# The step-by-step state-space recurrence of a hybrid block, issued on VectorE instead of GpSimd

## The chip, the core and the metric

One core of a Trainium2 chip runs the whole kernel. The metric is the device time of one execution in microseconds (us). Its engines are TensorE (PE in the profile, with PEld for its weight loads), VectorE (DVE), ScalarE (ACT), GpSimd (POOL) and SyncE (SP), each of which works through its own queue of instructions in order; DMA queues are fed from SP, ACT and POOL.

## What is computed

The reference is one layer of a diffusion backbone on 256 context and 256 latent tokens of width 2048: a token mixer with three branches (a Hyena long convolution, a chunkwise mLSTM, and an S5 state-space model), merged and projected, and then an MLP. The change touches the S5 branch. Each of its 48 groups has 64 complex states that run over the tokens in both directions:

```
def s5_direction(u, ab_re, ab_im, bb_re, bb_im, c_re, c_im, x0, readout):
    bu_re = jnp.einsum('blgc,gpc->blgp', u, bb_re)
    bu_im = jnp.einsum('blgc,gpc->blgp', u, bb_im)
    ...
    _, _, s_re, s_im = lax.associative_scan(s5_combine, (a_re, a_im, bu_re, bu_im), axis=1)
    ...
    y = (jnp.einsum('blgp,gcp->blgc', s_re, c_re.astype(F32))
         - jnp.einsum('blgp,gcp->blgc', s_im, c_im.astype(F32)))
```

The scan is x[n] = A x[n-1] + B u[n], with A diagonal and complex.

## The kernel before

**Matrix products.** Every large product streams its weights from HBM in chunks of 128x1024 float32 (512 KB). A chunk is loaded by SP into a tile `wr` (four buffers). ACT rounds it into `wh` (line 190), DVE subtracts to get the rest, `wl` (line 194, function `split`); `wh` and `wl` have three buffers each. PE then multiplies with `wh` and `wl` (line 211): in the stage of this change a chunk feeds 24 matmuls of 128x256. A `wr` buffer can be loaded again when DVE has made its `wl`; a `wl` buffer can be written again when PE has used it.

**Side work.** Generators are woven into the chunks: after each chunk a side advances by a given rate. One side, `mod_late`, loads further 512 KB tiles of `w_mod` into the same `wr` buffers and accumulates them on DVE into `mac` (lines 1178 and 1180, two instructions for each tile). 

**The S5 branch.** Tokens are grouped by eight, so that 512 tokens give 64 columns (`NCH`). `s5_inject` writes all inputs of the recurrence into the tile `S` (a `t32` tile, `t` in the profile), 128 partitions by 2 directions x 2 parts (real, imaginary) x 24 x 64 columns; the column is innermost, so one column of `S` is 96 elements that lie 64 elements (256 bytes) apart. `s5_scan` (lines 642 to 655) then takes 63 steps of four instructions of 128x96 each. The temporaries `sc1` and `sc2` (both `sc` in the profile) are contiguous. `s5_output` reads the states into a block matrix `xb` (`b` in the profile; four copies by ACT and four products by DVE, line 679, for each of six column tiles), and PE reads `xb` with the matmuls of line 686.

**Where it runs.** In `run`, stage pB: six chunks of the Hyena projection (`hy`), `s5_inject`, then the scan as side 0 at rate 2, so that its 63 steps are woven into the next 32 chunks (30 of `hy`, 2 of the merge gates `mg`); 30 more chunks of `mg` are issued, then `s5_output` at rate 0.6 over the following 16 and more. At ends of blocks of `hy`, ACT copies the product out of PSUM, ACT and DVE apply a short convolution (lines 740 and 742), and POOL issues a DMA into `HX`; at ends of blocks of `mg`, ACT copies into `mg` tiles and POOL issues a DMA into `MG`.

**Order.** Within each engine the order of instructions is set when the kernel is built, by a scheduler that estimates how long each instruction takes on its engine. So an instruction that goes to another engine can also change the order of other work.

Of the kernel before, what the change touches and what calls it, by code (L numbers as in the profile page):

```python
# [115 lines left out]
class Kern:  # L116
# [526 lines left out]

    def s5_scan(self):

        v = self.nc.gpsimd
        S = self.S
        for n in range(1, NCH):
            t1 = self.t(self.sm, [P, 2, 2, 24], "sc1", 2)
            t2 = self.t(self.sm, [P, 2, 2, 24], "sc2", 2)  # L650
            v.tensor_mul(t1, self.a8[:, 0], S[:, :, :, :, n - 1])  # L651
            v.tensor_mul(t2, self.a8[:, 1], S[:, :, ::-1, :, n - 1])  # L652
            v.tensor_add(t1, t1, S[:, :, :, :, n])  # L653
            v.tensor_add(S[:, :, :, :, n], t1, t2)  # L654
            yield
# [917 lines left out]
```

## Time and profile before

| what | value |
|---|---|
| time, median of 3 runs | 2005.19 us (2005.02 to 2005.46) |
| the profiled execution, its time | 2014.18 us |
| the profiled execution, its span | 2012.4 us |
| mean granted TensorE clock | 0.966 |
| busy share of the span | PE 93%, PEld 85%, DVE 65%, ACT 40%, POOL 18% |

The profile is of one execution, 9 us above the median of the timed runs. All places below are in microseconds from the start of its span. A busy share is an average over stages with different limits.

### The profile page before, as it was taken

How to read it: one execution, taken by the hardware profiler on the slowest of the kernel's cores; microseconds unless marked ns; L12 is line 12 of the kernel's file. 1: busy time of each engine (PE TensorE's matmuls, PEld its weight loads, DVE VectorE, ACT ScalarE, POOL GpSimd, SP SyncE). 2: the span in 40 equal slices, each digit the busy share in tenths (PEclk: the TensorE clock that was granted, in tenths of full speed). 3: DMA queues.
4: the chain of work that ended last, by engine and by line, in shares of the span. 5: the costliest groups of instructions: out<-in, count | busy, mean ns of one | idle time of the engine just before them, and what ended most of it. 6: DMA issues, size and time to landing. Idle time of an engine off the chain costs nothing.

```text
span 2012.4 us, 34496 instructions
## 1 busy us (share of the span) xinstructions
PE 1870.4 (93%) x13945; PEld 1707.4 (85%) x13945; DVE 1300.5 (65%) x1810; ACT 803.2 (40%) x1063; POOL 361.7 (18%) x534
## 2 busy tenths in 40 slices
PE   5888999999997995999889998999999999999996
PEld 1666988989997995999779877999988899998985
DVE  8985777647866553556786866766755555555556
ACT  2433324226543333544234533444433344444332
POOL 1221101000019994000452400400000000000001
PEclk7898999999998997999999998999999999999998
DMA  9997667775797765677657866577765566666553
GB/s 346 339 344 262 192 202 220 227 208 174 232 349 230 239 222 210 226 254 259 244 180 253 276 225 227 158 240 224 254 224 187 187 183 186 181 186 231 190 188 105
DMA packets 253472, 455.92 MB, mean 227 GB/s; under 512 B 28597, under 2 KB 75349, under 8 KB 251776
## 3 DMA queue, kind: packets, MB, share of 16 engines
q1 hardware_dynamic: 221824, 382.43, 59.4%
q0 software_dynamic: 14112, 50.83, 7.0%
q10 hardware_dynamic: 17376, 20.45, 3.1%
q8 instruction: 109, 1.79, 0.4%
q14 instruction: 51, 0.42, 0.1%
HBM read 424.75 MB, written 32.05 MB: 227 GB/s over the span
## 4 chain that ended last, share of the span: by engine, by line
PE 67%; DMA 10%; DVE 9%; POOL 8%; issue 3%; ACT 2%; SPq 0%; ACTq 0%; POOLq 0%; DVEq 0%
PE mm L211 59%; PE aux L211 4%; DMA wr<-in_w_mod_dram 4%; DVE wl L194 3%; DMA wr<-in_w_in_dram 2%; POOL sc L651 2%; POOL sc L653 2%; POOL sc L652 2%; POOL t L654 2%; DMA wr<-in_w_out_dram 1%; ACT wh L190 1%; PE px L406 1%; PE px L211 1%; PE aux L214 1%; DVE mac L1180 1%
## 5 line engine op out<-in xcount | busy, mean ns | idle before, releaser
L211 PE MATMUL mm<-t,wh 128*128 128x256 f32 x5888 | 1101.7, 288 | 29.0 <-ACT wh L190 18.1
L211 PEld LDWEIGHTS mm<-t,wh 128*128 128x128 f32 x5888 | 932.2, 194 | 49.6 <-ACT wh L190 19.9
L194 DVE TENSOR_TENSOR wl<-wr,wh 128x1024 fp32r<-128x1024 f32 (+1 forms) x517 | 649.6, 1263 | 385.9 <-ACT wh L190 385.4
L190 ACT ACTIVATE wh<-wr 128x1024 fp32r<-128x1024 f32 (+1 forms) x517 | 545.9, 1058 | 811.0 <-PE mm L211 580.6
L211 PE MATMUL mm<-t,wl 128*128 128x256 f32 x2944 | 847.6, 288 | 13.9 <-DVE wl L194 13.8
L211 PEld LDWEIGHTS mm<-t,wl 128*128 128x128 f32 x2944 | 570.1, 194 | 25.9 <-DVE wl L194 18.3
L1180 DVE SCALAR_TENSOR_TENSOR mac<-wr,vecs,mac 128x512 f32<-128x512 f32 x240 | 185.3, 772 | 156.5 <-DMA wr<-in_w_mod_dram 153.8
L211 PE MATMUL mm<-wh,t 128*128 128x512 f32 (+1 forms) x960 | 249.1, 349 | 0.2
L211 PEld LDWEIGHTS mm<-wh,t 128*128 128x128 f32 x960 | 169.0, 190 | 24.2 <-ACT wh L190 1.6
L211 PE MATMUL mm<-wl,t 128*128 128x512 f32 (+1 forms) x480 | 168.0, 350 | 5.5 <-DVE wl L194 5.5
L211 PE MATMUL mm<-wh,ff 128*128 128x512 f32 (+1 forms) x576 | 155.3, 358 | 0.0
L211 PEld LDWEIGHTS mm<-wh,ff 128*128 128x128 f32 x576 | 101.7, 188 | 17.6
L211 PEld LDWEIGHTS mm<-wl,t 128*128 128x128 f32 x480 | 91.3, 190 | 20.5 <-DVE wl L194 9.2
L211 PE MATMUL mm<-wl,ff 128*128 128x512 f32 (+1 forms) x288 | 103.0, 357 | 0.0
L211 PE MATMUL mm<-ty,wh 128*128 128x256 f32 x384 | 73.3, 289 | 0.0
L1402 POOL DMA_DIRECT2D t<-in_ln_g_dram x1 | 0.5, 535 | 355.0 <-PE mm L211 355.0
L211 PE MATMUL mm<-ty,wl 128*128 128x256 f32 x192 | 56.4, 294 | 7.6 <-DVE wl L194 7.5
L211 PEld LDWEIGHTS mm<-wl,ff 128*128 128x128 f32 x288 | 54.2, 188 | 8.8
L211 PEld LDWEIGHTS mm<-ty,wh 128*128 128x128 f32 x384 | 60.7, 192 | 0.9
L406 PE MATMUL px<-wr,b 128*32 128x512 f32 x128 | 41.4, 739 | 18.1 <-DVE s5t L335 10.5
L211 PE MATMUL aux<-t,t 128*128 128x384 f32 (+3 forms) x160 | 47.3, 411 | 7.7 <-DVE t L1146 3.2
L211 PEld LDWEIGHTS mm<-ty,wl 128*128 128x128 f32 x192 | 36.9, 192 | 9.1 <-DVE wl L194 8.4
(384 smaller groups left out, 1621.6 us busy)
## 6 DMA issues: line engine op xcount, KB each, us to landing
wr<-in_w_ff_dram SPq DMA_DIRECT2D x256, 512.0 KB, 3.9
wr<-in_w_in_dram SPq DMA_DIRECT2D x192, 512.0 KB, 4.7
wr<-in_w_mod_dram SPq DMA_DIRECT2D x160, 512.0 KB, 4.8
wr<-in_w_out_dram SPq DMA_DIRECT2D x32, 512.0 KB, 4.7
wh<-in_w_mod_dram SPq DMA_DIRECT2D x16, 512.0 KB, 7.6
wl<-in_w_mod_dram SPq DMA_DIRECT2D x16, 512.0 KB, 7.1
QD<-s5Q POOLq DMA_DIRECT2D x12, 512.0 KB, 7.1
WA<-s5wa POOLq DMA_DIRECT2D x24, 256.0 KB, 6.2
```

The lines of the kernel that those rows point to most:

```text
L190: return self.nc.scalar.activation(out, in_, f, bias=bias, scale=scale)
L194: self.nc.vector.tensor_sub(lo, x, hi.bitcast(F32))
L211: self.nc.tensor.matmul(out, lhsT, rhs, start=start, stop=stop, skip_group_check=True)
L214: self.nc.tensor.transpose(out, in_, self.c("ident", n)[:, :n])
L406: nc.tensor.matmul(ps[o:o + 32], self.st[:, k, :], raw[:, kk, :], start=k < 4, stop=k >= KT - 4, skip_group_check=True, tile_position=(0, o))
L651: v.tensor_mul(t1, self.a8[:, 0], S[:, :, :, :, n - 1])
L652: v.tensor_mul(t2, self.a8[:, 1], S[:, :, ::-1, :, n - 1])
L653: v.tensor_add(t1, t1, S[:, :, :, :, n])
L654: v.tensor_add(S[:, :, :, :, n], t1, t2)
L1180: v.scalar_tensor_tensor(acc, x, c, acc, op0=ALU.mult, op1=ALU.add)
L1402: nc.gpsimd.dma_start(g2r, I["ln2_g"].to_broadcast([P, D]))
```

## The change

One line: the four instructions of each step of the scan go to VectorE.

```
     def s5_scan(self):
 
-        v = self.nc.gpsimd
+        v = self.nc.vector
         S = self.S
         for n in range(1, NCH):
             t1 = self.t(self.sm, [P, 2, 2, 24], "sc1", 2)
             t2 = self.t(self.sm, [P, 2, 2, 24], "sc2", 2)
             v.tensor_mul(t1, self.a8[:, 0], S[:, :, :, :, n - 1])
             v.tensor_mul(t2, self.a8[:, 1], S[:, :, ::-1, :, n - 1])
             v.tensor_add(t1, t1, S[:, :, :, :, n])
             v.tensor_add(S[:, :, :, :, n], t1, t2)
             yield
```

All 252 instructions leave POOL and stand on DVE, between its `wl`, `mac` and convolution instructions. Here are twelve rows of the DVE queue in the stage of `mg`, with the difference marked; `sc_...` are the scan's temporaries, `t_677` is `S`, `wl_7379` and `wl_7409` are two consecutive chunks.

```order
 L194 TENSOR_TENSOR wl_7379<-wr_7376,wh_7378 128x1024
+L651 TENSOR_TENSOR sc_814_6190<-t_677_5292 128x96
+L652 TENSOR_TENSOR sc_815_6191<-t_677_5292 128x96
+L653 TENSOR_TENSOR sc_814_6190<-sc_814_6190,t_677_5292 128x96
+L654 TENSOR_TENSOR t_677_5292<-sc_814_6190,sc_815_6191 128x96
+L651 TENSOR_TENSOR sc_816_6196<-t_677_5292 128x96
+L652 TENSOR_TENSOR sc_817_6197<-t_677_5292 128x96
+L653 TENSOR_TENSOR sc_816_6196<-sc_816_6196,t_677_5292 128x96
 L194 TENSOR_TENSOR wl_7409<-wr_7406,wh_7408 128x1024
-L1180 SCALAR_TENSOR_TENSOR mac_7371<-wr_7496,vecs_93,mac_7371 128x512 x2
+L654 TENSOR_TENSOR t_677_5292<-sc_816_6196,sc_817_6197 128x96
+L1180 SCALAR_TENSOR_TENSOR mac_7371<-wr_7496,vecs_93,mac_7371 128x512
```

Eight instructions of the scan come between the two chunks and their `mac` pair, and the pair is split. PE's queue moves too: where the first matmuls of `s5_output` (line 686) stood, the products of the chunk `wh_8472` (an `mg` chunk) now run on.

```order
 L211 MATMUL mm_8110<-t_20_103,wh_8389 128x256 x2
 L211 MATMUL mm_8110<-t_20_103,wl_8390 128x256
-L211 MATMUL mm_8110<-t_20_103,wh_8472 128x256
-L686 MATMUL aux_8200<-s5wq_8190,b_1109_8182 64x128 x16
-L692 MATMUL aux_8200<-s5tp_8188,b_1111_8186 32x128 x8
-L211 MATMUL mm_8110<-t_20_103,wh_8472 128x256
+L211 MATMUL mm_8110<-t_20_103,wh_8472 128x256 x2
 L211 MATMUL mm_8110<-t_20_103,wl_8473 128x256
 L211 MATMUL mm_8110<-t_20_103,wh_8472 128x256 x2
```

They stand 90 matmuls of 128x256 later, in the middle of the chunk `wh_8679`, where the fourth column tile of `s5_output` was before.

```order
 L211 MATMUL mm_8593<-t_20_103,wl_8680 128x256
 L211 MATMUL mm_8593<-t_20_103,wh_8679 128x256
-L211 MATMUL aux_8460<-consts_91,b_1110_8184 128x32 x8
-L686 MATMUL aux_8514<-s5wq_8504,b_1109_8182 64x128 x16
-L692 MATMUL aux_8514<-s5tp_8502,b_1143_8500 32x128 x8
+L686 MATMUL aux_8200<-s5wq_8190,b_1109_8182 64x128 x16
+L692 MATMUL aux_8200<-s5tp_8188,b_1111_8186 32x128 x8
 L211 MATMUL mm_8593<-t_20_103,wh_8679 128x256
 L211 MATMUL mm_8593<-t_20_103,wl_8680 128x256
```

Each of the other column tiles moves back by the same 90 matmuls. Counted from the last matmul of `s5_inject`, the first matmul of line 686 came after 1123 products before, and comes after 1213 now. ACT's copies into `xb` move with them; SP's queue is unchanged; POOL's queue keeps its DMAs in their order.

## Rows read from the trace of the kernel before

**Rows 1.** The page: 40 slices (busy, granted clock in tenths), chain shares by engine.

```profile
PE   5888999999997995999889998999999999999996
...
PEclk7898999999998997999999998999999999999998
...
PE 67%; DMA 10%; DVE 9%; POOL 8%; issue 3%; ACT 2%; SPq 0%; ACTq 0%; POOLq 0%; DVEq 0%
```

**Rows 2.** Waits, 560 to 850 us: engine, line, waited for; us in total, times, longest.

```profile
PE aux L686 <- POOL sc L651: 21.4, 1, 21.4
...
ACT wh L190 <- DMA HX<-b: 11.8, 1, 11.8
...
ACT mg L190 <- DMA MG<-mg: 6.3, 1, 6.3
```

**Rows 3.** Line 651: duration ns min/median/max, first and last start us, forms.

```profile
L651 POOL TENSOR_TENSOR sc<-t x63: 431/449/1454, 601.8 to 776.2; 128x96 f32<-128x96 f32 x63
```

**Rows 4.** Windows of 20 us: busy us and instructions by engine, PEclk, DMA share, GB/s.

```profile
600.00:620.00 20.00, 15.39 (x112) 14.90 (x111) 12.24 (x17) 8.68 (x14) 15.33 (x27) 0.85 0.74 254
...
660.00:680.00 20.00, 20.00 (x169) 20.00 (x168) 10.97 (x10) 8.36 (x9) 18.97 (x29) 1.00 0.75 237
...
760.00:780.00 20.00, 2.91 (x28) 2.94 (x30) 3.30 (x6) 3.76 (x9) 16.66 (x41) 0.52 0.07 27
```

**Rows 5.** Chain that ended last, in order of time: start us, us, what.

```profile
597.19 6.00 PE mm L211 x50
...
777.09 3.68 PE aux L686 x32
...
787.14 1.90 PE aux L686 x32
...
826.97 38.83 PE mm L211 x323
```

**Rows 6.** Timeline of DVE, a recurrence of 128x48 operations: start us, us, what.

```profile
14.98 0.24 DVE L477 TENSOR_TENSOR s5t<-s5pq 128x48 f32<-128x48 f32 x1
15.15 0.23 DVE L478 TENSOR_TENSOR s5t<-s5pq 128x48 f32<-128x48 f32 x1
15.42 0.24 DVE L479 TENSOR_TENSOR s5pq<-s5t 128x48 f32<-128x48 f32 x1
15.70 0.24 DVE L480 TENSOR_TENSOR s5t<-s5pq 128x48 f32<-128x48 f32 x1
15.86 0.23 DVE L481 TENSOR_TENSOR s5t<-s5pq 128x48 f32<-128x48 f32 x1
```

**Rows 7.** DVE by form, whole span: busy us, mean ns, idle before.

```profile
L725 DVE TENSOR_TENSOR z<-z,b 128x256 f32<-128x256 f32 x6 | 2.2, 418 | 0.0
...
L479 DVE TENSOR_TENSOR s5pq<-s5t 128x48 f32<-128x48 f32 x7 | 1.7, 245 | 0.2
...
L496 DVE TENSOR_TENSOR s5t<-s5t 128x48 f32<-128x48 f32 x1 | 0.2, 207 | 0.0
```

**Rows 8.** DVE by form, 600 to 780 us.

```profile
L194 DVE TENSOR_TENSOR wl<-wr,wh 128x1024 fp32r<-128x1024 f32 x47 | 64.8, 1406 | 21.5 <-ACT wh L190 21.5
```

**Rows 9.** Timeline of DVE, 830 to 900 us, where POOL computes nothing.

```profile
838.13 0.75 DVE L1180 SCALAR_TENSOR_TENSOR mac<-wr,vecs,mac 128x512 f32<-128x512 f32 x1 [1.77 <-DMA wr<-in_w_mod_dram]
838.79 1.22 DVE L194 TENSOR_TENSOR wl<-wr,wh 128x1024 fp32r<-128x1024 f32 x1
...
888.69 3.52 DVE L194 TENSOR_TENSOR wl<-wr,wh 128x1024 fp32r<-128x1024 f32 x3
```

**Rows 10.** Timeline of DVE around the first step of the recurrence.

```profile
601.54 0.35 DVE L641 TENSOR_TENSOR t<-aux,one 128x64 f32<-128x64 f32 x2
...
604.95 0.48 DVE L742 SCALAR_TENSOR_TENSOR b<-b,vecs,b 128x252 f32<-128x252 f32 x1
605.38 1.23 DVE L194 TENSOR_TENSOR wl<-wr,wh 128x1024 fp32r<-128x1024 f32 x1
```

**Rows 11.** DMA issues, 600 to 780 us: count, KB each, median us to landing.

```profile
wr<-in_w_mod_dram SPq DMA_DIRECT2D x14, 512.0 KB, 5.1
```

More of the change, by code (lines that the diff above doesn't have):

```diff
@@ L644, in s5_scan @@
     def s5_scan(self):
-        v = self.nc.gpsimd
+        v = self.nc.vector
         S = self.S
```

## The prediction

> **What bounds the kernel now.** First the page: PE is busy in nine tenths of most slices, and the chain that ended last runs 67% through PE, but 8% of it through POOL. One slice in the middle, the sixteenth, falls to 5 tenths [rows 1]. The waits of that stretch name the cause: PE stood 21.4 us before the first matmul of line 686, for the last step of the scan on POOL [rows 2]. The scan ran from 601.8 to 776.2 us [rows 3], and the windows show POOL busy for up to 19 of 20 us while PE does almost nothing from 760 to 780 and its granted clock averages 0.52 there [rows 4]. So here the scan on POOL ended last, not PE. Its median instruction takes 449 ns but its longest 1454 [rows 3].
>
> Two smaller losses of the stretch hang on the same queue. POOL also issues the DMAs of `HX` and `MG`; ACT waited 11.8 and 6.3 us for buffers that these DMAs were to free [rows 2], since they were queued behind scan instructions.
>
> **What is removed.** POOL computes nothing in the stretch any more, so the 21.4 us go as far as DVE is not as late, and the DMAs are issued when their data is there. The unit of comparison is the start of line 686: before, at 777.1 us [rows 5], after 1123 products of `mm`. The changed queue of PE puts it after 1213. A product takes 38.83/323 = 0.120 us on a full PE [rows 5], so before, the same amount of work was done at 777.1 + 90 x 0.120 = 787.9 us. The first set of 32 matmuls of line 686 took 3.68 us, a later one 1.90 [rows 5]: PE came out of the wait at half its granted clock (1.2 instead of 2.4 GHz). Without the wait 1.8 us more are won: **the mark to beat is 789.7 us**.
>
> **What is added on DVE.** The trace has no 128x96 instruction on DVE that steps through memory. The nearest is another recurrence, 128x48, whose elements lie 36 bytes apart: 245 ns, against 207 ns for a contiguous 128x48 [rows 7], so 37 ns for 48 elements, 0.78 ns each. A contiguous 128x256 takes 418 [rows 7], so 48 more elements cost 48 x (418 - 207)/208 = 49 ns. A scan instruction: 207 + 49 + 96 x 0.78 = **331 ns**. All four kinds have at least one operand in `S`, so all pay. From the starts in the same recurrence, an instruction that doesn't need the one just before it starts 0.16 to 0.17 us after it, 0.08 sooner than the duration; one that does starts 0.27 to 0.28 after it, 0.04 later [rows 6]. So 0.25 and 0.37 us from start to start.
>
> Counted in the changed order from the first scan instruction to the last product of line 679 for the first column tile:
> - 251 scan instructions, of which 74 are directly followed by one that needs them: 74 x 0.37 + 177 x 0.25 = 71.6 us.
> - 47 `wl` at 3.52/3 or a little less, 1.15 [rows 9]: 54.0. While POOL computed, they took 1406 ns each [rows 8], against 1.22 without it [rows 9]: this price is the one without.
> - 28 `mac` at 838.79 - 838.13 = 0.66 [rows 9]: 18.5.
> - 14 convolution instructions at 605.38 - 604.95 = 0.43 [rows 10]: 6.0.
> - eight small ones, priced as a scan instruction, 0.25: 2.0.
>
> Sum 152.1 us. DVE also waits. A `mac` pair needs its `w_mod` tile, whose load starts when DVE frees the `wr` buffer four tiles earlier, and takes 5.1 us [rows 11]. Six of the pairs stand only 3.4 to 4.1 us of DVE work behind that point (22.3 us together): 6 x 5.1 - 22.3 = 8.3 us. Behind the waiting `mac` stand the scan and the next `wl`, and PE waits for that. Together 160.4 us. The scan can start as before, after the last copy of line 641 at 601.9 [rows 10], so line 686 starts at about 762.5.
>
> PE alone would be there sooner: 1213 products from 597.2 us [rows 5], 145.6 us, and the 4.6 us that it stood at the end of a `hy` block between 600 and 620 [rows 4], which are ACT's and stay, with some 2 us of clock (0.85 in that window): 750 us. So **DVE becomes the bound of the stretch**, with 152 us of work in 160, and PE, some nine tenths busy, waits a little before most chunks. I take off 2 us more for the ends of the three `hy` blocks, where DVE cannot run ahead (nothing to 3 us). The gain: 789.7 - 762.5 - 2 = **25 us**. Afterwards PE is full up to 866 (38.83 us of products without a gap) [rows 5] and no DVE work is added, so nothing gives it back. From the profiled execution, 2014.2 - 25 = 1989; it was 9 us above the median of the runs, so the median goes from 2005.2 to **1980**.
>
> **The unknown price, from both sides.** `S` steps by 256 bytes, not 36. Below: if such steps cost nothing, a scan instruction takes 256 ns, the sum is 134 us and the waits some 10, and PE at 750 is the bound: gain 39, 1966. Above: as on POOL, 449 ns [rows 3], 0.37 and 0.49 from start to start: 101.8 us of scan, 182 with the rest, some 4 of waits: 788 us, gain 0 to 2. I take the value of the rows with the same kind of access on the same engine.
>
> The Trainium skill speaks against the change here (Vector Engine (DVE) Microarchitecture Reference, 5.2 Measured stream behaviour on trn2): a port keeps its full rate only for runs of at least two adjacent words; single words that hop cost about 1.7 ns each instead of 1.05, and in one case, a step of 24 words, 2.5. By its 1.7 the estimate is 0.32 us for an instruction, which the 128x48 rows bear out at 0.78 ns extra; by its 2.5 it is 0.40, and the time about 1993. No run yet shows which of them a step of 64 words pays.
>
> **The rivals.**
> 1. *PE stays the bound.* The steps are cheap or hidden, gain 33 to 39, 1966 to 1972. For it: contiguous rows of 207 ns. Against: every row with steps pays. Chance 0.10.
> 2. *The longer step costs more.* Halfway between 331 and 449 ns, 0.39: 0.31 and 0.43 from start to start, 86.7 us of scan, 167 with the rest, 6 of waits: 775, gain 13, 1992. Nothing in the rows excludes it. Chance 0.17.
> 3. *Slower: DVE is saturated.* The scan sits between `wl`s, which PE needs every 24 x 0.120 = 2.88 us; five of its instructions fall on each. Without them DVE needs 80.5 us for the stretch; to reach the mark at 789.7 it may take 187.8, so with 4 of waits 103 us are left for 251 instructions, 0.41 each from start to start, against 0.285 forecast. Beyond that the kernel is slower by 2.5 us for each 0.01: at 0.45, 10 us, 2015. For it: PE now hangs on DVE for 160 us, and a `mac` or convolution that waits holds up everything. Against: no DVE row of this size comes near. Chance 0.09.
> 4. *No change.* The time won is lost again later, or the price is as on POOL: 2005. Chance 0.04, since the stretch behind is PE's alone.
>
> **How the numbers follow.** The forecast has 0.60 (1976 to 1987), the rivals 0.10, 0.17, 0.09 and 0.04. 1980 is that of the likeliest case. A range of 1968 to 1996 leaves out half of rival 1 (0.05) and rivals 3 and 4 (0.13), and so 0.18. Faster by over 0.2% (4 us, about what a measurement of this kernel tells from no change): 0.60 + 0.10 + 0.17 = 0.87, less 0.01 for the edge of rival 2: 0.86. Same 0.05, slower 0.09.
>
> **What the changed profile would show.** No wait of PE for line 686 above 1 or 2 us; scan instructions on DVE with a mean near 0.33 us; DVE busy above 90% from 602 to 762; `wl` back at 1.23 us; many short waits of PE for `wl` (about 10 us in sum) with the clock still near 1; ACT's waits for `HX` and `MG` gone; line 686 first at 760 to 766, and the rest of the span shifted as a block. It is wrong if the scan's mean is above 0.4 us, if the short waits bring PE's clock down over the stretch, or if the wait for line 686 comes back with DVE as its releaser.

## The result, and the profile after

The median of the changed kernel is 1984.16 us (1979.80 to 1987.72, four runs) against 2005.11 (2004.02 to 2005.46, four runs): a ratio of 0.9896 with a 95% interval of 0.9879 to 0.9914. The forecast was 1980. The profiled execution after took 1979.8 us, the fastest of its four, while that of before took 2014 (in later comparisons the kernel before ran from 2000.6 to 2016.6 us), so spans are not compared below; stretches between the same instructions are.

The page of the changed kernel, the lines that answer to [rows 1]:

```profile
PE   5887999999998999999889998999999999999996
...
PEclk7888999999999999999999998999999999999998
...
PE 69%; DVE 13%; DMA 12%; issue 3%; ACT 2%; POOL 0%; ACTq 0%; POOLq 0%; DVEq 0%
```

The slice with 5 tenths is gone, and so is POOL's share of the chain; DVE's has grown from 9 to 13%.

The waits of the changed kernel from 560 to 850 us, against [rows 2] (engine, line, waited for; us in total, times, longest):

```profile
DVE mac L1180 <- DMA wr<-in_w_mod_dram: 28.0, 16, 8.8
...
PE mm L211 <- DVE wl L194: 8.2, 8, 1.5
...
PE mm L211 <- ACT wh L190: 3.2, 1, 3.2
PE aux L211 <- DVE z L701: 2.6, 1, 2.6
```

PE no longer waits for line 686, and ACT no longer for `HX` or `MG`. A wait of 2.6 us behind line 701 is new. The eight short waits for `wl` are not: the same view of the kernel before has, beside the 21.4 us for the scan,

```profile
PE mm L211 <- ACT wh L190: 8.4, 2, 5.3
...
PE mm L211 <- DVE wl L194: 6.4, 8, 1.4
```

So from the scan's start to line 686 PE stood 21.4 + 8.4 + 6.4 = 36.2 us before and 8.2 + 3.2 = 11.4 us after: 24.8 us less, while its waits for `wl` grew by only 1.8.

The scan and the output of the changed kernel by line (duration ns min/median/max, first and last start us), against [rows 3]:

```profile
L651 DVE TENSOR_TENSOR sc<-t x63: 317/332/344, 596.7 to 755.3; 128x96 f32<-128x96 f32 x63
...
L686 PE MATMUL aux<-s5wq,b x192: 272/273/418, 757.3 to 803.2; 128*64 128x128 f32 x192
```

DVE of the changed kernel by form, from the first scan instruction to the first of line 686 (busy us, mean ns, idle before), against [rows 8]:

```profile
L194 DVE TENSOR_TENSOR wl<-wr,wh 128x1024 fp32r<-128x1024 f32 x47 | 57.3, 1220 | 0.0
L1180 DVE SCALAR_TENSOR_TENSOR mac<-wr,vecs,mac 128x512 f32<-128x512 f32 x28 | 21.0, 749 | 10.8 <-DMA wr<-in_w_mod_dram 10.6
L651 DVE TENSOR_TENSOR sc<-t 128x96 f32<-128x96 f32 x63 | 20.9, 332 | 1.5
```

These are the terms of the forecast's sum: 47 `wl`, 28 `mac`, an instruction of 332 ns where 331 was forecast, waits for the modulation's tiles of 10.6 us where 8.3 was. Line 686 comes 757.3 - 596.7 = 160.6 us after the scan's start; 160.4 had been worked out. The chain that ended last, from 590 to 770 us, runs 33% through loads of `w_mod` tiles, 18% through `wl`, 18% through PE's products and 15% through the scan: DVE's queue ended last there, and its waits for `mac` tiles are the largest part of it.

Windows of the changed kernel, against [rows 4] (window, its length, then busy us and instructions of PE, PEld, DVE, ACT, POOL; PEclk, DMA share, GB/s):

```profile
660.00:680.00 20.00, 19.12 (x157) 18.92 (x158) 18.53 (x44) 8.40 (x9) 1.07 (x2) 1.00 0.74 234
...
760.00:780.00 20.00, 19.58 (x218) 18.56 (x217) 7.74 (x15) 11.21 (x24) 0.00 (x0) 1.00 0.99 369
780.00:800.00 20.00, 17.86 (x192) 16.70 (x192) 10.16 (x20) 7.93 (x19) 0.54 (x1) 0.91 0.74 231
```

From 660 to 680 DVE is nearly full and PE loses about 1 us in 20. From 780 to 800 something is given back. DVE's timeline there (start us, us, what, in brackets the idle time before and what ended it):

```profile
778.73 1.54 DVE L1180 SCALAR_TENSOR_TENSOR mac<-wr,vecs,mac 128x512 f32<-128x512 f32 x2 [8.83 <-DMA wr<-in_w_mod_dram]
780.19 1.22 DVE L194 TENSOR_TENSOR wl<-wr,wh 128x1024 fp32r<-128x1024 f32 x1
781.33 0.67 DVE L701 SCALAR_TENSOR_TENSOR z<-ty,vecs,aux 128x256 f32<-128x256 f32 x1
```

A `mac` waits 8.83 us for its tile while the output's loads keep the DMA engines at 0.99 of their time; line 701 stands behind it on DVE, PE waits 2.6 us for that, and its granted clock averages 0.91 in the window.

As a measure that needs no equal spans, take the time from the first scan instruction to DVE's first product of the merge (line 1233). Before it is 1080.3 - 601.8 = 478.5 us, after 1051.1 - 596.7 = 454.4: 24.1 us less. From there to the end of the span it is 932.1 and 926.9, and ahead of the scan 601.8 and 596.7; the unchanged kernel's runs differ by more than that. So the gain lies in the stretch, as forecast, and the medians give 21.

### The profile page after: what moved, and what is told of

The parts are those of the page before. It is cut to its first block, busy times and chain, and to the rows that moved or that the text cites. A ratio compares the mean times of both kernels' runs of the same rounds, so it can differ in the third digit from the quotient of the medians.

```text
span 1978.0 us, 34489 instructions
## 1 busy us (share of the span) xinstructions
PE 1866.6 (94%) x13945; PEld 1703.1 (86%) x13945; DVE 1352.4 (68%) x2062; ACT 803.2 (41%) x1063; POOL 207.5 (10%) x282
## 4 chain that ended last, share of the span: by engine, by line
PE 69%; DVE 13%; DMA 12%; issue 3%; ACT 2%; POOL 0%; ACTq 0%; POOLq 0%; DVEq 0%
PE mm L211 61%; DMA wr<-in_w_mod_dram 7%; DVE wl L194 5%; PE aux L211 4%; DVE mac L1180 1%; ACT wh L190 1%; PE px L211 1%; PE px L406 1%; PE aux L214 1%; DVE t L194 1%; DMA wr<-in_w_out_dram 1%; DMA s5wq<-WA 1%; DMA wr<-in_w_in_dram 1%; DMA wr<-in_w_hy_out_dram 1%; DMA wr<-in_w_ff_dram 1%
## 5 line engine op out<-in xcount | busy, mean ns | idle before, releaser
L211 PE MATMUL mm<-t,wh 128*128 128x256 f32 x5888 | 1099.2, 288 | 21.2 <-ACT wh L190 10.8
L194 DVE TENSOR_TENSOR wl<-wr,wh 128x1024 fp32r<-128x1024 f32 (+1 forms) x517 | 642.8, 1246 | 366.6 <-ACT wh L190 365.9
L211 PEld LDWEIGHTS aux<-t,t 128*128 128x128 f32 (+1 forms) x160 | 24.7, 198 | 16.6 <-issue 10.1
```

Source lines behind the costliest of these rows:

```text
L194: self.nc.vector.tensor_sub(lo, x, hi.bitcast(F32))
L211: self.nc.tensor.matmul(out, lhsT, rhs, start=start, stop=stop, skip_group_check=True)
```

## The experiments

The theory was: before, the end of the scan on POOL sets line 686; after, PE is held by DVE's own time, which is now the bound of the stretch. The rivals: the gain is that POOL's queue is free for the DMAs; it is only that the order puts line 686 later on PE; or DVE's work matters little. All ratios are against the kernel before, run on the same chip in the same series (its medians 2005 to 2009), so two kernels of the table are compared by their ratios rather than by their medians.

| kernel | median us | ratio, 95% interval | scan to line 1233, us | line 1233 to end, us |
|---|---|---|---|---|
| before | 2005.11 | 1 | 478.5 | 932.1 |
| changed | 1984.16 | 0.9896, 0.9879 to 0.9914 | 454.4 | 926.9 |
| e1 side by side, DVE | 1976.68 | 0.9846, 0.983 to 0.9862 | 448.8 | 929.8 |
| e2 side by side, POOL | 2006.03 | 0.9999, 0.9984 to 1.0014 | 474.0 | 927.9 |
| e3 one step | 1973.51 | 0.9821, 0.98 to 0.9842 | 442.3 | 929.6 |
| e4 a direction each | 2001.33 | 0.9967, 0.9949 to 0.9985 | 471.6 | 928.2 |
| e5 later output, POOL | 2008.1 | 0.9998, 0.9985 to 1.0011 | 480.3 | 928.5 |
| e6 no `mac` in the scan, POOL | 2018.7 | 1.0049, 1.0033 to 1.0066 | 485.5 | 943.6 |
| e7 no `mac` in the scan, DVE | 1988.84 | 0.9908, 0.9882 to 0.9933 | 450.2 | 945.9 |
| e8 side by side, no `mac` | 2017.45 | 1.0047, 1.0032 to 1.0063 | 444.2 | 985.9 |
| e9 `HX` on SP, POOL | 2009.06 | 1.0008, 0.9994 to 1.0022 | 479.4 | 927.8 |
| e10 six instructions, DVE | 1984.5 | 0.9885, 0.987 to 0.9901 | 457.6 | 926.1 |
| e11 side by side, `mac` early | 1993.49 | 0.9924, 0.991 to 0.9939 | 440.8 | 953.5 |
| e12 the same, `mac` spread | 1979.74 | 0.9854, 0.9836 to 0.9871 | 441.5 | 942.1 |

The last two columns are of one profiled execution each: the start of the first scan instruction, that of DVE's first product of line 1233 (1234 in e10, which has a line more), and the span's end. Between the two marks lie 123 chunks, but 126 in e6 to e8 and 125 in e11 and e12; three chunks are 72 products or 8.6 us of PE, two are 5.8 us, and by that much these five stretches are long beside the others.

**e1 and e2, the layout of `S`.** The same edit to the changed kernel and to the one before:

```diff
-        self.S = sx[:, :6144].rearrange("p (a b c d) -> p a b c d", a=2, b=2, c=24)
+        self.S = sx[:, :6144].rearrange("p (d a b c) -> p a b c d", a=2, b=2, c=24)
```

> The changed kernel with S laid out so that one chunk's 96 numbers lie side by side: the same instructions of the scan on VectorE read and write words in a row instead of one word every 256 bytes. If VectorE's own time is what bounds the stretch (the theory), the scan instruction falls from 331 to about 256 ns (207 + 49, the 75 ns of hopping gone), 251 x 0.075 = 19 us less of VectorE's work; TensorE then bounds the stretch at its own work, line 686 comes 5 to 9 us earlier against the scan's start, and the whole takes 1975 to 1980 us. If something else holds the stretch (TensorE's work alone, or the waits for the modulation's weights), the instruction falls but the time stays within 3 us of the changed kernel's 1984. If a hop costs nothing, 331 ns stays and so does the time. The writes of the lines 633 to 637 hop instead, which may give back 1 to 3 us in the injection.

> The kernel before, its scan left on GpSimd, with the same side-by-side layout of S. If GpSimd's instruction pays for the hops as VectorE's does, its median falls from 449 to about 370 ns, 251 x 0.075 = 19 us less of the scan, TensorE's wait of 21.4 us at line 686 shrinks to 2 to 5 us and the whole takes 1987 to 1992 us: then most of the gain needs no change of engine. If GpSimd's time is its start-up and its sharing with VectorE's work (instructions up to 1454 ns), the median moves by under 20 ns, the wait stays at 15 us or more and the time within 6 us of 2005.

Line 651 of e1, then that of e2:

```profile
L651 DVE TENSOR_TENSOR sc<-t x63: 249/257/263, 596.4 to 749.5; 128x96 f32<-128x96 f32 x63
```

```profile
L651 POOL TENSOR_TENSOR sc<-t x63: 387/396/1448, 600.2 to 761.4; 128x96 f32<-128x96 f32 x63
```

On DVE the hop cost 332 - 257 = 75 ns, the term of the forecast to the nanosecond, and without it the kernel takes 1976.7 us, the lowest median here of the kernels that make every step. On POOL the median falls too, by 53 ns, and the scan ends 13 us sooner after its start; but its longest instruction stays at 1448 ns, and the time doesn't move. The wait stays as long:

```profile
PE aux L686 <- POOL sc L652: 22.1, 1, 22.1
```

The order of this kernel puts line 686 74 matmuls, or 74 x 0.120 = 8.9 us, earlier, so PE came to the wait sooner by most of what the scan had gained. 4.5 us are left in the stretch, which the timing doesn't show.

**e3, one step.** All but the first of the 63 steps (the text on record says 62) are left out:

```diff
-        for n in range(1, NCH):
+        for n in range(1, 2):
```

> The changed kernel with one of the recurrence's 62 steps (it leaves the other steps out, so the chunks' states aren't carried on). It shows what TensorE alone would take for the stretch. If VectorE bounds the stretch by a few us (the theory: its work ended at 762.5, TensorE's at about 750), line 686 comes 6 to 12 us earlier for the same matmuls and the time is 1972 to 1978 us. If TensorE has no wait left, the time stays within 3 us of 1984. If the scan still costs much more than its stretch shows (a rival: VectorE's slowed weight splits), the time falls under 1968.

It took 1973.5 us. By the ratios that is 0.75% or 15 us below the changed kernel, and in the stretch 12.1 us: what the scan on DVE still costs. e1 gets back 10 us by the ratios, whose intervals don't meet, and 5.6 in the stretch.

**e5, the order alone.** The scan stays on POOL, line 686 is issued later:

```diff
-                self.run_steps(steps, 32)
+                self.run_steps(steps, 44)
                 self.with_side(self.s5_output(), 0.6)
-                self.run_steps(steps, 48)
+                self.run_steps(steps, 36)
```

> The kernel before, its scan left on GpSimd, with the output of the state-space stage issued 12 merge-gate steps later (44 and 36 in place of 32 and 48), which puts 191 more matmuls ahead of the first of line 686 on TensorE. If the gain of the change is TensorE's wait of 21.4 us and nothing else, 191 x 0.120 = 23 us of other work covers it here too, and the time is 1983 to 1988 us, as with the change. If the gain comes from GpSimd's queue or from VectorE and GpSimd no longer sharing a port, the weight splits stay at 1.4 us, the late HX and MG transfers stay, and only 8 to 14 us are won: 1991 to 1997. If the covered wait comes back elsewhere (the output's own chain has less work beside it), under 5 us are won.

No gain at all. ACT's timeline, and then PE's waits from 590 to 880 us, show where the covered wait went:

```profile
771.27 0.51 ACT L190 ACTIVATE b<-t 64x128 f32<-64x128 f32 x2 [25.43 <-POOL t L654]
```

```profile
PE mm L211 <- ACT wh L190: 26.8, 4, 18.7
```

ACT's copies of `S` for the output had not moved as far as PE's matmuls. They stood in ACT's queue, waiting for the scan's end, `wh` stood behind them, and PE stopped 18.7 us for `wh` in place of 21.4 at line 686. Other work covers a late producer only if no engine that this work needs is parked behind it.

**e9, POOL's queue alone.** The scan stays on POOL; the `HX` transfers of line 1086 go to SP's queue:

```diff
-                self.nc.gpsimd.dma_start(self.HX[2, :, ct * T:(ct + 1) * T], f)
+                self.nc.sync.dma_start(self.HX[2, :, ct * T:(ct + 1) * T], f)
```

> The kernel before, scan on GpSimd, with the six HX transfers of line 1086 issued from SP's queue, so that they no longer stand behind the scan on GpSimd's. ScalarE's wait of 11.8 us for HX and TensorE's stop of 5.3 us behind it should go either way. If part of the change's gain is that GpSimd's queue is free, 4 to 6 us are won here: 1999 to 2002 us. If the end of the scan alone sets line 686 (the theory), TensorE only arrives earlier and waits longer there; 57 fewer matmuls stand ahead of line 686, so 0 to 7 us are lost: 2005 to 2013.

ACT's wait for `HX` is gone, and from 640 to 660 us PE is busy for 20.00 us where it was 14.07 before:

```profile
640.00:660.00 20.00, 20.00 (x169) 20.00 (x169) 13.03 (x13) 8.40 (x9) 19.14 (x28) 1.00 0.79 254
```

Yet the time is that of before: PE arrives sooner, behind 57 matmuls fewer, and waits for the scan:

```profile
PE aux L686 <- POOL sc L651: 19.4, 1, 19.4
```

ACT's waits for `MG` are longer here, 22.3 us in three. So neither the order nor this part of the queue carries the gain; the end of the scan does. The `MG` transfers were not taken off POOL's queue by themselves.

**e6, what makes POOL late.** In the kernel before, no `mac` beside the scan:

```diff
-                self.sides[1][1] = 0.3
+                self.sides[1][1] = 0.0
                 self.with_side(self.s5_scan(), 2)
...
+                self.sides[1][1] = 0.3
                 self.with_side(self.s5_output(), 0.6)
...
                 self.s5_glu()
+                self.sides[1][1] = 0.6
```

> The kernel before, scan on GpSimd, with none of the modulation's multiply-adds (line 1180) in the scan's stretch; they are made up after the state-space stage. If GpSimd's scan is long because VectorE's instructions hold it up (174 us where 251 x 0.443 = 111 would do), taking 27 x 0.85 = 23 us of them away shortens it by 10 to 20 us, and the wait at line 686 with it: 1988 to 1998 us. If the scan is long for a reason of its own, its instructions' mean stays at 640 ns and the time at 2005.

The scan is hardly shorter: 589.0 to 762.7 us, 173.7 in place of 175.9. But two windows, and the two timelines from 655 us, show what lengthens it:

```profile
680.00:700.00 20.00, 20.00 (x169) 20.00 (x168) 8.40 (x7) 8.24 (x9) 18.94 (x31) 1.00 0.62 185
...
740.00:760.00 20.00, 0.00 (x0) 0.00 (x0) 0.00 (x0) 0.00 (x0) 18.39 (x46) 0.55 0.16 53
```

```profile
655.43 1.42 POOL L653 TENSOR_TENSOR sc<-sc,t 128x96 f32<-128x96 f32 x1
...
658.41 1.44 POOL L652 TENSOR_TENSOR sc<-t 128x96 f32<-128x96 f32 x1
```

```profile
655.14 1.42 DVE L194 TENSOR_TENSOR wl<-wr,wh 128x1024 fp32r<-128x1024 f32 x1 [1.36 <-ACT wh L190]
658.02 1.53 DVE L194 TENSOR_TENSOR wl<-wr,wh 128x1024 fp32r<-128x1024 f32 x1 [1.46 <-ACT wh L190]
```

With DVE idle POOL does 46 instructions in 20 us, with seven `wl` beside it 31, its DMA issues among them. An instruction held up by a `wl` takes up to 1.4 us, to about 0.3 us past the end of that `wl`. The Trainium skill (SBUF — State Buffer, SBUF: two separate sides) says that DVE and GpSimd lock a shared pair of ports for a whole instruction, also where the DVE instruction has two SBUF inputs and the GpSimd one reads SBUF, and that the other then stands still; the trace agrees.

A part of the expectation was wrong: most of the lengthening is the work of `wl`, which PE needs, and less that of `mac`. A `mac` does hold POOL up, as the timelines of POOL and DVE in the kernel before show; the instruction takes 0.90 us, again to 0.3 us past the end:

```profile
659.35 0.90 POOL L653 TENSOR_TENSOR sc<-sc,t 128x96 f32<-128x96 f32 x1
```

```profile
659.00 0.93 DVE L1180 SCALAR_TENSOR_TENSOR mac<-wr,vecs,mac 128x512 f32<-128x512 f32 x1
```

But with 20 `mac` fewer beside it the scan had 48 `wl` beside it in place of 44, and line 686 came after 74 matmuls more. So e6 does not show what the `mac` alone cost the scan. The made-up `mac` cost more than was freed.

**e4, half on each engine.** The forward direction on DVE, the backward one on GpSimd, in the changed kernel:

```diff
+            for d, v in enumerate((self.nc.vector, self.nc.gpsimd)):
...
+                v.tensor_mul(t1, self.a8[:, 0, d], S[:, d, :, :, n - 1])
```

> The changed kernel with the forward direction of the recurrence on VectorE and the backward one on GpSimd, each in instructions of 48 numbers instead of 96. If VectorE's own time bounds the stretch (the theory), its scan instruction falls from 331 to about 245 ns, 251 x 0.086 = 21 us less, and the time goes to 1975 to 1980 us. If the two engines slow each other when both work, as the long GpSimd instructions of the kernel before suggest (up to 1454 ns beside a weight split that takes 1406 in place of 1220), the splits go back to 1.4 us and GpSimd's half takes 120 to 150 us, and 1983 to 1992 comes out.

2001.3 us: the theory's number was wrong, and the rival's was too good. The groups of line 651 of both halves (busy us, mean ns, idle before), and PE's waits from 590 to 880 us:

```profile
L651 POOL TENSOR_TENSOR sc<-t 128x48 f32<-128x48 f32 x63 | 32.6, 518 | 7.7 <-DVE t L641 3.2
...
L651 DVE TENSOR_TENSOR sc<-t 128x48 f32<-128x48 f32 x63 | 18.7, 297 | 1.3
```

```profile
PE mm L211 <- DVE wl L194: 18.1, 11, 3.0
PE mm L211 <- ACT wh L190: 7.5, 2, 4.3
```

Half the numbers cost DVE nearly the whole price (297 ns in the mean, where 245 was expected and the fastest took 228, against 332 for the whole), while GpSimd's take 518 with a median of 338. Both scan halves suffer when the other engine works, PE waits 18.1 us for `wl` in place of 8.2, and ACT waits 11.2 us for `HX` again.

**e7 and e8, `mac` out of the stretch.** e7 is the edit of e6 in the changed kernel. e8 has e1's layout, leaves `mac` out of the output as well, and sets the 0.6 behind it.

> The changed kernel, also with no multiply-adds of the modulation in the scan's stretch, made up after the state-space stage. If VectorE bounds the stretch (the theory), it loses 18.5 us of work and 8 to 14 us of waits for the modulation's weights, ends 133 us after the scan's start, and TensorE alone bounds it, as with one step of the recurrence: 1973 to 1978 us. If the multiply-adds only fill gaps that VectorE has anyway, the time stays at 1984 within 3; if making them up later costs, it is 1986 or more.

> The side-by-side layout of S and the modulation's multiply-adds left out of both the scan and the state-space output, made up afterwards. The theory: the floor of TensorE's own work in the stretch, and no wait of 8.8 us for a modulation tile beside the output's loads: 1969 to 1975 us, 2 to 6 below the layout alone. If the layout alone has already made TensorE the bound, 1975 to 1979.

In e7 the scan runs from 588.1 to 725.8 us, 137.7 in place of 161.8, and PE's waits for `wl` from 590 to 880 fall to one:

```profile
PE mm L211 <- DVE wl L194: 1.2, 1, 1.2
```

So in the stretch DVE, with its `mac` and their tiles, was what held PE. But the `mac` come back: line 1233 to the end takes 19 us longer in e7, 59 in e8, among whose waits of PE from 1050 to 1500 us are 31.9 us for `wh` and 8.8 for a `mac`. e8 ended 41 us slower than e1, and e7 no faster than the changed kernel. For e7 that is the last case of the expectation; e8's range was missed.

**e10, more work on DVE.** Both products of a step are made twice:

```diff
-            v.tensor_mul(t1, self.a8[:, 0], S[:, :, :, :, n - 1])
-            v.tensor_mul(t2, self.a8[:, 1], S[:, :, ::-1, :, n - 1])
+            for _ in range(2):
+                v.tensor_mul(t1, self.a8[:, 0], S[:, :, :, :, n - 1])
+                v.tensor_mul(t2, self.a8[:, 1], S[:, :, ::-1, :, n - 1])
```

> The changed kernel with the two products of every step made twice, six instructions of VectorE a step in place of four: 126 more at 0.25 to 0.37 from start to start, 31 to 46 us. The order puts 420 more matmuls (50 us) ahead of line 686, in which VectorE needs some 30 us for their splits. If VectorE bounds the stretch (the theory), its end moves from 161 to about 225 us after the scan's start while TensorE's own work ends near 198, and the whole loses 12 to 28 us: 1996 to 2012, so that the gain is gone at about six instructions. If VectorE still has room, under 6 us are lost: 1990 or less.

The expected loss did not come: 1984.5 us, and 3.2 us more in the stretch. DVE and PE of e10, then of the changed kernel, from 600 to 740 us:

```profile
600.00:740.00 140.00, 128.05 (x1027) 125.59 (x1027) 130.02 (x321) 53.91 (x61) 10.81 (x18) 0.98 0.75 238
```

```profile
600.00:740.00 140.00, 130.25 (x1043) 128.01 (x1042) 128.39 (x302) 54.17 (x61) 10.81 (x18) 0.98 0.76 240
```

DVE is no fuller and PE hardly emptier. The order spreads the longer scan over more of PE's work: line 686 comes 817.6 - 599.0 = 218.6 us after the scan's start, 58.0 later (64 was expected), and 416 more products, 49.9 us, are done ahead of it. For these DVE makes only 18 `wl` and 10 `mac` more, 29 us. So 8.1 us are lost at line 686; the give-back behind it (the 8.83 us of the changed kernel) is not there, and 3.2 are left at line 1233, where 12 to 28 were expected.

**e11 and e12, `mac` ahead of the scan.** e1 with

```diff
-                self.sides[1][1] = 0.6
+                self.sides[1][1] = 1.0
                 self.oT = self.ty()
...
-                self.sides[1][1] = 0.3
+                self.sides[1][1] = 0.1
                 self.with_side(self.s5_scan(), 2)
...
+                self.sides[1][1] = 0.3
                 self.with_side(self.s5_output(), 0.6)
```

and in e12 also 0.4 after `s5_glu`.

> The side-by-side layout with a third of the modulation's multiply-adds in the scan's stretch (a rate of 0.1 in place of 0.3) and more of them ahead of it (1.0 in place of 0.6 from the output gate on), so that none has to be made up later. If VectorE is still what the stretch waits for with the layout alone, 1 to 3 us more come: 1973 to 1976 us, the floor that one step gave. If the multiply-adds cost as much where they are put, the time is 1976 to 1985.

> The side-by-side layout with the modulation's multiply-adds thinned in the scan's stretch (0.1) and brought forward and spread after it (1.0 from the output gate, 0.4 after the state-space stage in place of 0.3), so that as many stand ahead of the feed-forward part as in the changed kernel: 204 of the 240, where the run with the same thinning but no spreading had 195. If that run lost its time to the 12 multiply-adds that its end made in one go, ahead of which ScalarE and TensorE stood 16 us, this one has no such stop and takes 1970 to 1976 us, at or a little below the layout alone (1976.7). If the multiply-adds cost as much wherever they stand, it is 1977 to 1985.

PE is full in the stretch in both; the window of e12:

```profile
600.00:740.00 140.00, 140.00 (x1170) 140.00 (x1169) 119.52 (x322) 59.87 (x69) 10.85 (x18) 1.00 0.79 242
```

Both are also 13 us shorter to line 1233 than the changed kernel, with two chunks more between the marks and fewer `mac` (56 in e11 and 63 in e12 for 70), and yet not faster than e1. In e11 the rest of the modulation is made in one go in the feed-forward part; DVE's timeline and ACT's:

```profile
1416.40 7.04 DVE L1180 SCALAR_TENSOR_TENSOR mac<-wr,vecs,mac 128x512 f32<-128x512 f32 x9
```

```profile
1426.58 1.06 ACT L190 ACTIVATE wh<-wr 128x1024 fp32r<-128x1024 f32 x1 [11.59 <-DMA wr<-in_w_ff_dram]
```

The modulation's tiles took the buffers and the queue of the weights, and PE stood 16.0 us. In e12 that stop is gone and the rest is given back in smaller waits: from 1040 to 1250 us PE waits 14.3 us for `wl`. Its 1979.7 (1972.5 to 1983.9) can't be told from e1's 1976.7 (1974.0 to 1977.0), nor was it below it as expected.

## Why the prediction was right, and where it was not

- **The wait for POOL sets the stretch: right.** PE's waits up to line 686 fell by 24.8 us. Taking away the queueing of `HX` (e9), the order (e5) or a part of POOL's own time (e2) gave nothing that the timing shows. The `HX` and `MG` waits were real, but hidden behind the scan's end.
- **The mark of equal work: right.** One rule fits seven of the kernels within 2 us: the time from the scan's start to line 686, less 0.120 us for each product that stands ahead of it beyond the 1123 of the kernel before. Before 175.3 us; changed 160.6 - 90 x 0.120 = 149.8, so 25.5 won where 25 was forecast and 24.1 is seen at line 1233. e1: 751.6 - 596.4 = 155.2 after the start, less 10.8, so 30.9 won and 29.7 seen. e2: 162.4 + 8.9, 4.0 won, 4.5 seen. e3: 129.0 + 11.6, 34.7 won, 36.2 seen. e4: 158.0 + 11.6, 5.7 won, 6.9 seen. e5: 199.7 - 22.9, 1.5 lost, 1.8 seen. e9: 168.5 + 6.8, nothing won, 0.9 lost. e10 is off by 3.5 us. Where the `mac` were moved, the chunks more have to be allowed for (e7: 39.9 won by the rule, 28.3 + 8.6 = 36.9 seen), and in e6 the rule fails even so: 11 won by it, 1.6 seen.
- **The price of an instruction: right.** 331 forecast, 327 to 332 measured in the four lines. What the forecast left open, whether a hop of 256 bytes costs more than one of 36, is settled: 75 ns for 96 words, 0.78 each, in both. The Trainium skill (Vector Engine (DVE) Microarchitecture Reference, 5.2 Measured stream behaviour on trn2) has 1.7 ns for a hopping word and 2.5 in one case. The trace agrees with the first: a word costs 0.78 ns more in the changed kernel than in e1, where it would be 0.65 by the 1.7 and 1.45 by the 2.5.
- **DVE's sum and its waits: right, the last digits by luck.** The total was right to 0.2 us, but the waits for tiles were 10.6 us for 8.3 and the rest 160.6 - 10.6 = 150.0 for 152.1: two misses of over 2 us cancel. `wl` is back at 1220 ns; DVE is busy for 147 of the 160 us from 600 to 760.
- **"DVE becomes the bound of the stretch": right, but by less than was said.** The chain runs through DVE's queue there, and PE's waits for `wl` up to line 686 fall from 8.2 us to 5.3 in e1, 2.5 in e3 and 1.2 in e7. But PE was to wait "a little before most chunks", and it waited before 8 of 47, as often as before the change. In e1, with the same 1213 products ahead of line 686, DVE is busy for 17 us less (130.2 for 147.2) and line 686 comes only 5.4 us sooner.
- **Rival 3's rule, the gain gone at 0.41 us from start to start: not tested.** e10 adds 126 x 0.25 = 31.5 us, which for 251 instructions is 0.285 + 0.125 = 0.41, and the medians show no loss. But the rule holds the order fixed, with 1213 products ahead of line 686, and e10 has 416 more, in whose 49.9 us DVE has some 20 us to spare. PE loses much the same share of its time: 148.6 of 160 us busy from 600 to 760 in the changed kernel (7.1% lost), 203.3 of 220 from 600 to 820 in e10 (7.6%). The expectation for e10 failed by its size: line 686 came 6 us sooner than was summed, and of the 8.1 us lost there 4.9 came back behind it. Dearer instructions in the changed kernel's own order, as in rivals 2 and 3, were not tried.
- **"Nothing gives it back": off by 2.6 us and some clock.** The output's loads and a modulation tile now meet (the wait of 8.83 us above), in a stretch that was counted as PE's alone. That takes the 25.5 us at line 686 to 24.1 at line 1233. What is left between 24.1 and the 21 of the medians, and between the forecast's 1980 and 1984, is no more than the changed kernel's own runs differ by, 1979.8 to 1987.7; no place in the trace was found for it.
- **"4.6 us at the end of a `hy` block are ACT's and stay": too strong.** They are there in the changed kernel (PE 15.33 of 20 us from 600 to 620, clock 0.83) and in e3, but in e7, e8, e11 and e12, where the `mac` are thinned and the order around the block differs, PE is busy for 20.00 of 20. Which of the two removes them was not tried apart.

## What to carry to other kernels

Ask which engine ends last and what is parked in order behind it on the others: here neither a freer queue nor covering work helped while ACT and DVE stood behind the scan, and moving the scan did. Before moving work to a busier engine, price it from rows of the same access pattern on that engine, then look at the layout: putting the 96 numbers side by side was one line and gave a quarter (in the stretch) to a half (by the ratios) of the change's own gain again. And where more instructions also move the order, count the work that comes with them: in e10, the one run that tried it, 31.5 us more on DVE cost 3.2 us in the stretch.

## What the runs showed of the hardware that was not expected

- A GpSimd instruction that meets a `wl` on DVE waits that instruction out: 1.42 us in place of 0.44 (e6), and `wl` itself goes from 1220 to 1406 ns. A `mac` does the same, to 0.90 us. The scan of 252 instructions then takes 174 us on GpSimd, where 46 in 20 us, its pace with DVE idle, would give 110.
- Side by side, GpSimd's instruction falls from 449 to 396 ns and DVE's from 332 to 257: the hop costs both, by 53 and 75 ns for 96 words.
- Half an instruction is no half price when both engines share the work: 128x48 took 285 to 320 ns (means of the four lines) on DVE beside GpSimd's scan, where the same shape, at a step of 36 bytes, took 245 in the kernel before [rows 7] and 128x96 took 327 to 332 without GpSimd.
